# A searched planned order, a root planned step by step, and value projections of 512 columns in a hybrid attention and SSD encoder layer

## The chip, the cores and the metric

The kernel runs on one core of one Trainium2 chip. The core has five instruction queues that run side by side and meet at semaphores: TensorE (PE; its weight loads are shown as PEld), VectorE (DVE), ScalarE (ACT), GpSimd (POOL) and SyncE (SP, which issues the DMAs). The metric is the time of one execution in microseconds (us) on the device. The kernel before takes 1236.46 us, the median of three runs (1235.29 to 1237.94).

## What is computed

One encoder layer on a sequence of 512 tokens with 1024 channels, all in float32:

```
h = layer_norm(x)
proj = h @ w_in                      # q | k | v | z | x_ssd B C | dt | gates
ya = neighbourhood_attention(q, k, v, rpb) @ w_attn_br
xbc = silu(centred_dwconv(x_ssd B C))          # 5 taps, 4096 channels
y = ssd(forward) + ssd(backward) + xs * d_skip  # 8 groups, chunks of 128 tokens
y = y * silu(z);  y = y * rsqrt(mean(y*y over a group's 256) + 1e-5) * ssd_norm_w
ys = y @ w_ssd_br
h = layer_norm(alpha * h + (sigmoid(gate_a) * ya + sigmoid(gate_s) * ys) @ w_o)
h = layer_norm(alpha * h + relu(h @ w_ff1)**2 @ w_ff2)
```

## The kernel before

**Matmuls.** Every large product is done with operands split in two float32r parts, high and low. `mm3` (L305 to L308) issues three matmuls for one tile of 128 contracted channels: high times high (L306), low times high (L307), high times low (L308). Weights come in slabs of 128 x 2048 elements: a DMA into `ws`, a rounded copy into `wh` on ACT and the rest into `wl` on DVE or POOL, with two buffers of each.

**Stages.** First comes the stage that a planner orders: the first norm, the SSD branch over eight groups and the first gates. Then follow the values of the attention (L1053 to L1067), q and k and the attention head by head, the branch projection, the merge, the output projection, and the MLP. The planned stage ends, and the values begin, at 522 us of the profile.

**The planner.** In the planned stage no line issues its instruction at once. `op(engine, us, fn, r, w)` records an operation with its engine, an assumed duration and what it reads and writes. `Plan.order` (L106) then plays these operations as a list schedule: the rank of an operation is the longest assumed path behind it, each engine takes the ready operation of the highest rank, and on PE an operation marked `filler` (the projections) only where no other is ready. A hand-over between engines costs `LAT`, 0.2 us for all engines. An operation marked `lock` on DVE waits for one on POOL to end, and the other way round. `Plan.issue` (L251) plays 100 seeds, each of which multiplies the ranks by a random factor of up to 1.001, keeps the seed whose played end is earliest, and issues the operations in that order. The queues of the engines then run in order: an instruction that waits holds everything behind it on its engine. What is issued after the planned stage is ordered by the compiler's own scheduler.

**A group g of the SSD branch.** Four projections of 128 channels over 512 tokens go to PSUM (`ps_x`, 24 matmuls each, two banks called mm), are convolved (`cv`: ACT one tap, L686; DVE four taps, L694; ACT the silu, L697) and the last two are transposed (`tp_x`, L786). `bc` holds cumulated decays: a DMA from `acs_d` fills it, DVE and POOL subtract (L871), DVE merges the two directions with a predicated copy (L875), ACT takes the exponential (L877), DVE multiplies with `cb` (L879), and PE uses it as weights for `yd` (L885). z is projected with 96 matmuls of 256 columns (`ps_z`), into the same two mm banks. `gated_norm` (L921) multiplies y with z on POOL, squares on ACT, takes the inverse root of four numbers per partition on POOL, scales on ACT, transposes on PE (`tp_y`, L955) and splits into `yTh` (ACT, L958) and `yTl` (DVE, L960). `ssd_branch` multiplies these with `w_ssd_br` (`ps_sbr`) and DVE adds the result into `ysacc` (L981). The transposes `tp_b`, `tp_x` and `tp_y` share two PSUM banks called tr. Names carry the group: `tp_y5_1` is the second transpose of group 5, `cv6_1` the second convolution of group 6.

**The root.** Before, the sixteen instructions of the inverse root are one operation of the plan, with an assumed 3.7 us:

```
op("POOL", 3.7, f_rs, r=[(ssq.name, c) for c in range(NT)], w=[(ssq.name, "r")], lock=True)
```

**The values.** `hBh` and `hBl` are reordered copies of `hTh` and `hTl`, made by 16 DVE copies (L1051). Four slabs of 256 columns are multiplied with them, 4 x 4 x 8 x 3 = 384 matmuls `ps_v`, two blocks of 256 columns to an mm bank; ACT and DVE split each block into `vhl` (L1066, L1067).

Of the kernel before, what the change touches and what calls it, by code (L numbers as in the profile page):

```python
# [19 lines left out]
P = 128  # L20
# [42 lines left out]
SEEDS = 100  # L63
# [7 lines left out]
class Plan:  # L71
# [3 lines left out]
    LAT = 0.2  # L75
# [29 lines left out]
    def order(self, seed=0):  # L105
# [32 lines left out]
        for tag, ts in fixed.items():  # L138
            ts.sort(key=lambda t: first[t])
            for a, b in zip(ts, ts[self.tags[tag]:]):  # L140
                pred[first[b]].update(users[a])
        succ = [[] for _ in ops]
# [14 lines left out]
        for i in reversed(topo):  # L157
            rank[i] = ops[i]["us"] + max((rank[s] + (0 if ops[s]["e"] == ops[i]["e"] else self.LAT)
                                          for s in succ[i]), default=0.0)
# [24 lines left out]
        while done < n:  # L184
            while finish and finish[0][0] <= t:
                _, i = heapq.heappop(finish)
                done += 1
                for s in succ[i]:
                    deg[s] -= 1
                    lat = 0.0 if ops[s]["e"] == ops[i]["e"] else self.LAT  # L190
# [59 lines left out]

    def issue(self):  # L251

        best = None
        for seed in range(SEEDS):
            try:
                o = self.order(seed)
            except AssertionError:
                continue
            if best is None or max(self.end) < best[0]:
                best = max(self.end), o, self.start, self.end  # L260
        self.start, self.end = best[2:]
        for i in best[1]:
            self.ops[i]["fn"]()
# [3 lines left out]
def encoder_layer(ctx, tc, x, w_in, w_attn_br, w_ssd_br, w_o, w_ff1, w_ff2, pcols, rows64,  # L267
# [123 lines left out]
    def by_dir(t, c, g):  # L391
# [7 lines left out]
                 "t1": 2, "ssq": 1, "yTh": 1, "yTl": 1, "gt": 4})  # L399
# [108 lines left out]
    for half in range(2):  # L508
# [9 lines left out]
        for k in range(KD):  # L518
# [8 lines left out]
            if HMB_ENG[half][k] == "ACT":  # L527
                op("ACT", 0.4, lambda k=k, sl=sl, hb_=hb_: a_.activation(
                    hb_()[:, 0], hTh[:, k, sl].bitcast(F32), AF.Identity, bias=nb0[:, k : k + 1]),
                   r=[("hTh", k, half), ("nb0", 0)], w=[(hb_.name, 0)])  # L530
            elif HMB_ENG[half][k] == "DVE":
                op("DVE", 0.28, lambda k=k, sl=sl, bk=bk, hb_=hb_: v_.tensor_scalar(
                    out=hb_()[:, 0], in0=hTh[:, k, sl].bitcast(F32), scalar1=bk, scalar2=None,
                    op0=ALU.subtract), r=[("hTh", k, half)], w=[(hb_.name, 0)], lock=True)
# [4 lines left out]
            op("DVE", 0.43, lambda k=k, tpx=tpx, sl=sl, gk=gk, hb_=hb_: v_.scalar_tensor_tensor(  # L539
# [384 lines left out]
    def gated_norm(g, yz, sz):  # L924
# [12 lines left out]
        box = []  # L937

        def f_rs():
            nc.gpsimd.tensor_scalar(out=ssq(), in0=ssq(), scalar1=1.0 / 256.0, scalar2=None,  # L940
                                    op0=ALU.mult)
            box.append(rsqrt(sbp, ssq(), NT, f"rms{g}", eng=nc.gpsimd))
        op("POOL", 3.7, f_rs, r=[(ssq.name, c) for c in range(NT)], w=[(ssq.name, "r")], lock=True)
        for c in range(NT):
            op("ACT", 0.5, lambda c=c: nc.scalar.activation(yz()[:, c, :], yz()[:, c, :], AF.Copy,
                                                            scale=box[0][:, c : c + 1]),
               r=[(ssq.name, "r"), (yz.name, c)], w=[(yz.name, c)])
# [105 lines left out]
    for s in range(4):  # L1053
        wv = weights([(w_in, 0, OFF_V + s * 256, 256)], KD, 256, f"v{s}")
        for b2 in range(2):
            ps = psx.tile([P, 2, 256], F32, tag="mm", bufs=BANKS["mm"], name=f"ps_v{s}_{b2}")
            for j in range(2):
                bs = slice((2 * b2 + j) * P, (2 * b2 + j + 1) * P)
                for k in range(KD):
                    mm3(ps[:, j, :], hBh[:, k, bs], hBl[:, k, bs],  # L1060
                        wv[0][:, k, :], wv[1][:, k, :], k == 0, k == KD - 1)
            for j in range(2):
                b, prs = 2 * b2 + j, slice(2 * s, 2 * s + 2)
                pv4 = ps[:, j, :].rearrange("p (r h q) -> p r h q", r=2, h=2)
                hi = vhl[:, b, prs, 0:4:3, :]
                nc.scalar.activation(hi, pv4, AF.Copy)  # L1066
                nc.vector.tensor_tensor(out=vhl[:, b, prs, 1:3, :], in0=pv4, in1=hi.bitcast(F32),  # L1067
                                        op=ALU.subtract)
# [422 lines left out]
```

## Time and profile before

| what | value |
|---|---|
| median of three runs | 1236.46 us (1235.29 to 1237.94) |
| the profiled execution | 1234.04 us, of which the span from first to last instruction is 1232.3 us |
| granted TensorE clock, mean | 0.990 |
| PE busy | 1192.6 us, 97% |
| DVE, ACT, POOL busy | 753.9, 557.9, 487.7 us |
| the planned stage | 0 to 522 us |
| the values | 523.2 to 569.5 us |

A matmul of the profile is shown longer than its distance from the next one, since matmuls overlap: 256 columns are shown with 283 ns. The spacing is found by counting matmuls in a stretch in which PE never stops. The granted clock is 1.00 at 2.4 GHz and 0.50 at 1.2 GHz.

### The profile page before, as it was taken

The page shows a single profiled execution, that of the slowest core. Times are in us where ns is not written, and L with a number is a line of the kernel's source. Part 1 is how long each engine was busy: PE and PEld are TensorE (multiplying, and loading weights), DVE is VectorE, ACT ScalarE, POOL GpSimd, SP SyncE. Part 2 cuts the span into 40 slices and gives each one's busy share as a digit, 9 for nine tenths or more (in the row PEclk, how much of TensorE's full clock was granted, in tenths as well). Part 3 has the DMA queues.
Part 4 walks back from the last instruction along what each step waited for, and adds up shares of the span by engine and source line. Part 5 has one row for each costly group of instructions (what it writes and reads, how often), then busy time and mean ns, then how long its engine had stood idle before and what let it go on. Part 6 is the DMA issues. An engine that isn't in the chain of part 4 may idle for free.

```text
span 1232.3 us, 17117 instructions
## 1 busy us (share of the span) xinstructions
PE 1192.6 (97%) x6570; PEld 1029.3 (84%) x6570; DVE 753.9 (61%) x1369; ACT 557.9 (45%) x949; POOL 487.7 (40%) x540
## 2 busy tenths in 40 slices
PE   5999999999999999999999989999999999999997
PEld 5988888988887888799888878889988888888885
DVE  7758586565768486453789975357664343443556
ACT  5557573646545454423667782342232331331510
POOL 1167878686867585403567730015240000000000
PEclk8999999999999999999999999999999999999998
DMA  6153243333333322233333323354213333222401
GB/s 227 52 155 123 89 134 133 108 103 103 103 110 98 124 98 82 88 100 74 93 82 86 83 91 115 103 170 138 69 69 103 103 103 103 90 89 95 151 38 52
DMA packets 126498, 127.22 MB, mean 103 GB/s; under 512 B 22352, under 2 KB 109008, under 8 KB 126416
## 3 DMA queue, kind: packets, MB, share of 16 engines
q1 hardware_dynamic: 126416, 126.13, 32.6%
q8 instruction: 52, 0.85, 0.3%
q14 instruction: 30, 0.25, 0.1%
HBM read 123.88 MB, written 2.23 MB: 102 GB/s over the span
## 4 chain that ended last, share of the span: by engine, by line
PE 79%; DVE 12%; ACT 3%; issue 2%; DMA 2%; POOL 1%; SPq 0%; DVEq 0%; ACTq 0%; POOLq 0%
PE ps_f L308 9%; PE ps_f L307 9%; PE ps_f L306 9%; DVE cv L694 3%; PE ps_x L308 3%; PE ps_x L306 3%; PE ps_x L307 3%; PE yd L885 2%; PE ps_sbr L306 2%; PE ps_z L306 2%; DVE bc L875 2%; PE ps_sbr L308 2%; PE ps_sbr L307 2%; PE ps_z L307 2%; PE ps_z L308 2%
## 5 line engine op out<-in xcount | busy, mean ns | idle before, releaser
L295 ACT ACTIVATE wh_f<-ws_f 128x1024 fp32r<-128x1024 f32 x60 | 60.1, 1052 | 118.6 <-PE ps_f L307 96.4
L694 DVE SCALAR_TENSOR_TENSOR cv<-ps_x,pc,cv 128x510 f32<-128x510 f32 (+1 forms) x128 | 95.5, 748 | 28.0 <-ACT cv L686 24.8
L307 PE MATMUL ps_f<-h1Th,wl_f 128*128 128x512 f32 (+1 forms) x288 | 104.6, 366 | 0.0
L306 PE MATMUL ps_f<-h1Th,wh_f 128*128 128x512 f32 (+1 forms) x288 | 104.4, 366 | 0.0
L308 PE MATMUL ps_f<-h1Tl,wh_f 128*128 128x512 f32 (+1 forms) x288 | 103.1, 367 | 1.0 <-DVE h1Tl L382 1.0
L296 DVE TENSOR_TENSOR wl_f<-ws_f,wh_f 128x1024 fp32r<-128x1024 f32 x60 | 72.8, 1251 | 45.3 <-ACT wh_f L295 45.0
L307 PE MATMUL ps_f<-wh_f,gl 128*128 128x512 f32 x224 | 86.8, 389 | 0.0
L308 PE MATMUL ps_f<-wl_f,gh 128*128 128x512 f32 x224 | 86.5, 389 | 0.0
L306 PE MATMUL ps_f<-wh_f,gh 128*128 128x512 f32 x224 | 86.3, 389 | 0.0
L306 PE MATMUL ps_z<-wh_z,hTh 128*128 128x256 f32 x256 | 75.7, 296 | 2.6 <-DVE cv L694 2.6
L307 PE MATMUL ps_z<-wh_z,hTl 128*128 128x256 f32 x256 | 72.3, 283 | 0.0
L308 PE MATMUL ps_z<-wl_z,hTh 128*128 128x256 f32 x256 | 72.3, 283 | 0.0
L871 DVE TENSOR_TENSOR bc<-bc,amd 128x512 f32<-128x512 f32 x32 | 44.9, 1412 | 37.8 <-DMA bc<-acs_d 30.0
L1364 DVE TENSOR_TENSOR rl<-rl,ps_f 128x512 f32<-128x512 f32 x32 | 21.7, 687 | 69.0 <-ACT rl L1363 68.8
L306 PEld LDWEIGHTS ps_f<-h1Th,wh_f 128*128 128x128 f32 x288 | 54.1, 188 | 8.9
L307 PEld LDWEIGHTS ps_f<-h1Th,wl_f 128*128 128x128 f32 x288 | 54.2, 188 | 8.7
L308 PEld LDWEIGHTS ps_f<-h1Tl,wh_f 128*128 128x128 f32 x288 | 53.3, 188 | 9.8 <-DVE h1Tl L382 1.2
L1363 ACT ACTIVATE rl<-ps_f 128x512 f32<-128x512 f32 x32 | 19.0, 597 | 89.0 <-PE ps_f L308 85.5
L306 PE MATMUL ps_sbr<-yTh,wh_sbr 128*128 128x512 f32 x128 | 56.8, 443 | 1.0 <-DVE ysacc L981 0.9
L306 PE MATMUL ps_x<-hTh,wh_x 128*128 128x512 f32 (+1 forms) x144 | 56.1, 390 | 0.7 <-DVE cv L694 0.7
L306 PE MATMUL ps_x<-hTh,wh_bc 128*128 128x512 f32 (+1 forms) x144 | 56.0, 389 | 0.0
L307 PE MATMUL ps_x<-hTh,wl_bc 128*128 128x512 f32 (+1 forms) x144 | 53.9, 374 | 1.8 <-POOL wl_bc L427 1.8
(300 smaller groups left out, 3723.6 us busy)
## 6 DMA issues: line engine op xcount, KB each, us to landing
ws_f<-in_w_ff SPq DMA_DIRECT2D x32, 1024.0 KB
bc<-acs_d SPq DMA_DIRECT2D x32, 512.0 KB
ws_bc<-in_w_in SPq DMA_DIRECT2D x16, 512.0 KB
ws_x<-in_w_in SPq DMA_DIRECT2D x8, 1024.0 KB
ws_z<-in_w_in SPq DMA_DIRECT2D x8, 1024.0 KB
ws_g<-in_w_in SPq DMA_DIRECT2D x8, 1024.0 KB
ws_sbr<-in_w_ssd_br SPq DMA_DIRECT2D x8, 1024.0 KB
ws_qk<-in_w_in SPq DMA_DIRECT2D x16, 512.0 KB
```

Of the source, the lines that this page charges most:

```text
L295: nc.scalar.activation(hi[:, k], st[:, k], AF.Copy)
L296: (eng[i] if isinstance(eng, tuple) else eng).tensor_tensor(out=lo[:, k], in0=st[:, k], in1=hi[:, k].bitcast(F32), op=ALU.subtract)
L306: nc.tensor.matmul(o, lh, rh, start=start, stop=False)
L307: nc.tensor.matmul(o, ll, rh, start=False, stop=False)
L308: nc.tensor.matmul(o, lh, rl, start=False, stop=stop)
L694: op("DVE", 0.75, lambda j=j, o=o, n=n: nc.vector.scalar_tensor_tensor(out=acc()[:, o], in0=ps()[:, n], scalar=tap(j), in1=acc()[:, o], op ...
L871: op(e, us, lambda d=d, eng=eng, c=c, bc=bc: eng.tensor_tensor(out=bc()[:, d], in0=bc()[:, d], in1=by_dir(amd, c, g)[:, d, :].unsqueeze(2) ...
L875: op("DVE", 0.75, lambda bc=bc: nc.vector.copy_predicated(bc()[:, 0], msk, bc()[:, 1]), r=[(bc.name, 1), ("msk", 0)], w=[(bc.name, 0)], lo ...
L885: nc.tensor.matmul(yd()[:, c % 2, h * HD : (h + 1) * HD], bc()[:, 1, h, :], xtok()[:, c, h * HD : (h + 1) * HD], start=True, stop=True)
L1363: nc.scalar.activation(rl, ps, AF.Relu)
L1364: nc.vector.tensor_tensor(out=rl, in0=rl, in1=ps, op=ALU.mult)
```

## The change

1. `LAT` becomes a table by the engine that hands over: 0.18 us from PE, 0.06 from DVE, ACT and POOL, 0 from SP.
2. The 100 seeds go. `NUDGES` holds ten pairs of a seed and a spread; the ranks are multiplied by the random factors of all ten in turn, and the one order that comes of it is issued. `replay`, a second player that walks a given order in each engine's own sequence with durations lengthened at random, stands in the file and is not called when the kernel is built.
3. Three assumed durations of the first norm become longer (0.4 to 0.51, 0.28 to 0.35, 0.43 to 0.48 us).
4. The root becomes sixteen operations of the plan, 0.29 us each, with one buffer for each of its four tiles where there were two. They are the same sixteen instructions.
5. The values use two slabs of 512 columns, each in two halves of the contraction, in four PSUM banks (so, tr, so, tr): 2 x 2 x 4 x 4 x 3 = 192 matmuls of 512 columns, and 8 blocks of 512 columns to split where there were 16 of 256.

```
-    LAT = 0.2
+    LAT = {"PE": 0.18, "DVE": 0.06, "ACT": 0.06, "POOL": 0.06, "SP": 0.0}
...
-        if seed:
+        for seed, sigma in nudges:
             draw = random.Random(seed)
-            rank = [r * (1 + 0.001 * draw.random()) for r in rank]
+            rank = [r * (1.0 + sigma * draw.random()) for r in rank]
...
-        op("POOL", 3.7, f_rs, r=[(ssq.name, c) for c in range(NT)], w=[(ssq.name, "r")], lock=True)
+        def small(w, f, *r):
+            op("POOL", 0.29, f, r=[(rt[n].name, 0) for n in r], w=[(rt[w].name, 0)], lock=True)
...
-    for s in range(4):
-        wv = weights([(w_in, 0, OFF_V + s * 256, 256)], KD, 256, f"v{s}")
-        for b2 in range(2):
-            ps = psx.tile([P, 2, 256], F32, tag="mm", bufs=BANKS["mm"], name=f"ps_v{s}_{b2}")
...
+    for s in range(2):
+        pss = [psx.tile([P, 512], F32, tag=tag, bufs=BANKS[tag], name=f"ps_v{s}_{b}")
+               for b, tag in enumerate(("so", "tr", "so", "tr"))]
+        for k0 in (0, 4):
+            wv = weights([(w_in, k0 * P, OFF_V + s * 512, 512)], 4, 512, f"v{s}_{k0}")
+            for b in range(4):
+                bs = slice(b * P, (b + 1) * P)
+                for k in range(k0, k0 + 4):
+                    mm3(pss[b], hBh[:, k, bs], hBl[:, k, bs], wv[0][:, k - k0, :], wv[1][:, k - k0, :],
+                        k == 0, k == KD - 1)
```

The added lines move what follows them: in the changed kernel, the lines of the planned stage stand 46 further on (L871 is L917, L875 is L921, L694 is L740), those of the root's end and of `gated_norm` behind it 66 (L955 is L1021, L960 is L1026).

What the new order does on DVE between groups 5 and 6. Before, from the last tap of `cv6_0` on:

```order
L694 SCALAR_TENSOR_TENSOR cv6_0_3561<-ps_x6_0_3512,pc_82,cv6_0_3561 128x510
L694 SCALAR_TENSOR_TENSOR cv6_1_3616<-ps_x6_1_3552,pc_82,cv6_1_3616 128x510
L694 SCALAR_TENSOR_TENSOR cv6_1_3616<-ps_x6_1_3552,pc_82,cv6_1_3616 128x511 x2
L694 SCALAR_TENSOR_TENSOR cv6_1_3616<-ps_x6_1_3552,pc_82,cv6_1_3616 128x510
L875 COPY_PREDICATED bc6_2_3501<-msk_98,bc6_2_3501 128x512
L875 COPY_PREDICATED bc6_3_3509<-msk_98,bc6_3_3509 128x512
L960 SCALAR_TENSOR_TENSOR yTl5_3670<-tp_y5_0_3646,pc_82,yTh5_3660 128x512
L694 SCALAR_TENSOR_TENSOR cv6_2_3668<-ps_x6_2_3608,pc_82,cv6_2_3668 128x510
```

In the changed kernel, the same queue from the late subtractions of `bc6` on:

```order
L917 TENSOR_TENSOR bc6_3_3514<-bc6_3_3514,amd_101 128x512
L917 TENSOR_TENSOR bc6_1_3523<-bc6_1_3523,amd_101 128x512
L740 SCALAR_TENSOR_TENSOR cv6_0_3556<-ps_x6_0_3496,pc_82,cv6_0_3556 128x510
L740 SCALAR_TENSOR_TENSOR cv6_0_3556<-ps_x6_0_3496,pc_82,cv6_0_3556 128x511 x2
L740 SCALAR_TENSOR_TENSOR cv6_0_3556<-ps_x6_0_3496,pc_82,cv6_0_3556 128x510
L921 COPY_PREDICATED bc6_1_3523<-msk_98,bc6_1_3523 128x512
L921 COPY_PREDICATED bc6_3_3514<-msk_98,bc6_3_3514 128x512
L740 SCALAR_TENSOR_TENSOR cv6_1_3597<-ps_x6_1_3552,pc_82,cv6_1_3597 128x510
```

and further down that queue, where group 5 is split:

```order
L849 TENSOR_TENSOR coef6_3722<-dt_100,cbd6_3702 128x16
L851 TENSOR_TENSOR coef6_3722<-coef6_3722,dsk_99 128x16
L740 SCALAR_TENSOR_TENSOR cv6_3_3714<-ps_x6_3_3648,pc_82,cv6_3_3714 128x510
L740 SCALAR_TENSOR_TENSOR cv6_3_3714<-ps_x6_3_3648,pc_82,cv6_3_3714 128x511 x2
L740 SCALAR_TENSOR_TENSOR cv6_3_3714<-ps_x6_3_3648,pc_82,cv6_3_3714 128x510
L1026 SCALAR_TENSOR_TENSOR yTl5_3766<-tp_y5_0_3717,pc_82,yTh5_3756 128x512
L1026 SCALAR_TENSOR_TENSOR yTl5_3766<-tp_y5_1_3727,pc_82,yTh5_3756 128x512
```

The two predicated copies moved from behind `cv6_1` to in front of it, and both splits `yTl5`, which stood on either side of `cv6_2`, moved together behind `cv6_3`.

On PE, where group 5 is transposed. Before, `tp_y5_1` stands within the projection `ps_x6_3`:

```order
L307 MATMUL ps_x6_3_3662<-hTh_69,wl_x6_3531 128x512
L308 MATMUL ps_x6_3_3662<-hTl_70,wh_x6_3521 128x512
L955 MATMUL tp_y5_1_3682<-cst_81,yz5_3473 128x128 x4
L306 MATMUL ps_x6_3_3662<-hTh_69,wh_x6_3521 128x512
L307 MATMUL ps_x6_3_3662<-hTh_69,wl_x6_3531 128x512
L308 MATMUL ps_x6_3_3662<-hTl_70,wh_x6_3521 128x512
L776 MATMUL cb6_3694<-cv6_1_3616,cv6_0_3561 128x128 x4
```

In the changed kernel both transposes stand together within the projection of z:

```order
L352 MATMUL ps_z6_0_3706<-wh_z6_3611,hTh_69 128x256
L353 MATMUL ps_z6_0_3706<-wh_z6_3611,hTl_70 128x256
L354 MATMUL ps_z6_0_3706<-wl_z6_3628,hTh_69 128x256
L1021 MATMUL tp_y5_0_3717<-cst_81,yz5_3484 128x128 x4
L1021 MATMUL tp_y5_1_3727<-cst_81,yz5_3484 128x128 x4
L352 MATMUL ps_z6_0_3706<-wh_z6_3611,hTh_69 128x256
```

Before, `tp_y5_0` and `tp_y5_1` were 15 projection matmuls apart; now they are neighbours, six matmuls of z in.

On PE, the start of the values. Before, two banks side by side:

```order
L306 MATMUL ps_v0_0_4723<-wh_v0_4715,hBh_4697 128x256
L306 MATMUL ps_v0_1_4776<-wh_v0_4715,hBh_4697 128x256
L307 MATMUL ps_v0_0_4723<-wh_v0_4715,hBl_4698 128x256
L308 MATMUL ps_v0_0_4723<-wl_v0_4716,hBh_4697 128x256
L307 MATMUL ps_v0_1_4776<-wh_v0_4715,hBl_4698 128x256
L308 MATMUL ps_v0_1_4776<-wl_v0_4716,hBh_4697 128x256
```

In the changed kernel, four banks side by side:

```order
L352 MATMUL ps_v0_0_4715<-wh_v0_0_4719,hBh_4697 128x512
L352 MATMUL ps_v0_1_4716<-wh_v0_0_4719,hBh_4697 128x512
L352 MATMUL ps_v0_2_4717<-wh_v0_0_4719,hBh_4697 128x512
L352 MATMUL ps_v0_3_4718<-wh_v0_0_4719,hBh_4697 128x512
L353 MATMUL ps_v0_0_4715<-wh_v0_0_4719,hBl_4698 128x512
L354 MATMUL ps_v0_0_4715<-wl_v0_0_4720,hBh_4697 128x512
L353 MATMUL ps_v0_1_4716<-wh_v0_0_4719,hBl_4698 128x512
L354 MATMUL ps_v0_1_4716<-wl_v0_0_4720,hBh_4697 128x512
```

Each stationary tile pair now meets 512 columns of weights at a time, and the first contracted tile serves four blocks of tokens before the second is needed.

## Rows read from the trace of the kernel before

**Rows 1.** The page's first part: busy time, share and instructions of each engine.

```profile
PE 1192.6 (97%) x6570; PEld 1029.3 (84%) x6570; DVE 753.9 (61%) x1369; ACT 557.9 (45%) x949; POOL 487.7 (40%) x540
```

**Rows 2.** Waits of PE: who waited for whom, us in total, times, longest.

```profile
PE tp_h L515 <- DVE xn L486: 10.0, 1, 10.0
PE tp_y L955 <- DVE yTl L960: 2.9, 1, 2.9
PE ps_z L306 <- DVE cv L694: 2.6, 3, 1.5
PE ps_x L307 <- POOL wl_bc L427: 1.8, 1, 1.8
PE tp_x L786 <- DVE yTl L960: 1.8, 1, 1.8
PE ps_v L306 <- ACT wh_v L295: 1.2, 1, 1.2
```

**Rows 3.** PE around 397 us: start, us, instruction, [idle before, releaser].

```profile
396.59 0.39 PE L308 MATMUL ps_x<-hTl,wh_x 128*128 128x512 f32 x1
399.89 1.12 PE L955 MATMUL tp_y<-cst,yz 128*128 128x128 f32 x4 [2.91 <-DVE yTl L960]
```

**Rows 4.** DVE from 379 to 400 us.

```profile
379.58 5.53 DVE L871 TENSOR_TENSOR bc<-bc,amd 128x512 f32<-128x512 f32 x2
...
390.82 3.11 DVE L694 SCALAR_TENSOR_TENSOR cv<-ps_x,pc,cv 128x510 f32<-128x510 f32 x4 [2.70 <-ACT cv L686]
393.85 5.36 DVE L875 COPY_PREDICATED bc<-msk,bc 128x512 f32<-128x512 int32 x2
399.11 0.73 DVE L960 SCALAR_TENSOR_TENSOR yTl<-tp_y,pc,yTh 128x512 fp32r<-128x512 f32 x1
```

**Rows 5.** Stretches: us, busy of each engine (count), granted clock, DMA.

```profile
380.00:400.00 20.00, 17.09 (x79) 13.58 (x78) 17.08 (x14) 12.76 (x23) 15.48 (x22) 0.98 0.22 62
400.00:420.00 20.00, 20.00 (x130) 18.89 (x131) 10.16 (x23) 10.67 (x13) 6.57 (x5) 0.85 0.37 129
```

**Rows 6.** PE around 181 us.

```profile
181.86 1.31 PE L786 MATMUL tp_x<-cst,cv 128*128 128x128 f32 x8 [1.80 <-DVE yTl L960]
```

**Rows 7.** DVE before it.

```profile
177.63 3.54 DVE L875 COPY_PREDICATED bc<-msk,bc 128x512 f32<-128x512 int32 x2
181.07 1.39 DVE L960 SCALAR_TENSOR_TENSOR yTl<-tp_y,pc,yTh 128x512 fp32r<-128x512 f32 x2
```

**Rows 8.** Stretches of 256-column matmuls alone, then of 512-column matmuls alone.

```profile
524.00:564.00 40.00, 40.00 (x336) 40.00 (x334) 18.29 (x33) 10.55 (x20) 0.00 (x0) 1.00 0.30 87
900.00:1000.00 100.00, 100.00 (x443) 82.84 (x442) 46.97 (x54) 32.81 (x45) 6.29 (x3) 1.00 0.30 95
```

**Rows 9.** PE where the planned stage ends and the values begin.

```profile
521.61 0.40 PE L308 MATMUL ps_sbr<-yTl,wh_sbr 128*128 128x512 f32 x1
523.22 0.47 PE L306 MATMUL ps_v<-wh_v,hBh 128*128 128x256 f32 x2 [1.21 <-ACT wh_v L295]
```

**Rows 10.** DVE at the same place.

```profile
522.05 0.69 DVE L981 TENSOR_TENSOR ysacc<-ps_sbr,ysacc 128x512 f32<-128x512 f32 x1 [0.69 <-PE ps_sbr L308]
522.66 0.42 DVE L1051 CAST hBh<-hTh 128x512 fp32r<-128x512 f32 x1
```

**Rows 11.** The splits of the values: durations in ns min/median/max, first and last start.

```profile
L1067 DVE TENSOR_TENSOR vhl<-ps_v,vhl x16: 418/424/427, 532.3 to 573.8; 128x256 fp32r<-128x256 f32 x16
```

**Rows 12.** POOL, the root of the last group, its first and last instruction.

```profile
498.66 0.23 POOL L940 TENSOR_SCALAR ssq<-ssq 128x4 f32<-128x4 f32 x1 [1.03 <-ACT sz L934]
...
503.00 0.20 POOL L329 TENSOR_TENSOR rs_y_rms<-rs_t_rms,rs_y_rms 128x4 f32<-128x4 f32 x1
```

**Rows 13.** Groups by line: count, busy us, mean ns, idle before.

```profile
L875 DVE COPY_PREDICATED bc<-msk,bc 128x512 f32<-128x512 int32 x32 | 48.2, 1536 | 0.2
L871 DVE TENSOR_TENSOR bc<-bc,amd 128x512 f32<-128x512 f32 x32 | 44.9, 1412 | 37.8 <-DMA bc<-acs_d 30.0 <-PE st L849 7.6
...
L877 ACT ACT_TABLE_LOAD x21 | 26.9, 1283 | 1.3 <-DVE bc L875 1.0
```

More of the change, by code (lines that the diff above doesn't have):

```diff
@@ L103, in op, with order @@
                              table=table, filler=filler, at=at))
-    def order(self, seed=0):
+    def order(self, nudges=()):
         ops, n = self.ops, len(self.ops)
@@ L249, in order, with replay @@
         return sorted(range(n), key=lambda i: (start[i], i))
-    def issue(self):
[L253 to L262, printed above, removed]
+    def replay(self, order, seed, spread):
+        ops, n = self.ops, len(self.ops)
+        at = {i: p for p, i in enumerate(order)}
+        pred = [set(p) for p in self.pred]
+        slots = {g: [None] * c for g, c in self.tags.items()}
+        for i in order:
+            for x in ops[i]["tiles"]:
+                u = self.users[x]
+                if i != min(u, key=at.get):
+                    continue
+                s = slots[self.tiles[x].tag]
+                k = min(range(len(s)), key=lambda j: s[j][0] if s[j] else -1.0)
+                if s[k]:
+                    pred[i].update(p for p in s[k][1] if at[p] < at[i])
+                s[k] = (max(self.end[p] for p in u), u)
+        draw = random.Random(seed)
+        queue = {}
+        for i in reversed(order):
+            queue.setdefault(ops[i]["e"], []).append(i)
+        free = dict.fromkeys(queue, 0.0)
+        lock = {"DVE": 0.0, "POOL": 0.0}
+        end, dma, table = [None] * n, 0.0, "sqrt"
+        for _ in range(n):
+            best = None
+            for e, q in queue.items():
+                if not q:
+                    continue
+                i = q[-1]
+                if any(end[p] is None for p in pred[i]):
+                    continue
+                t = max([free[e], ops[i]["at"]] + [
+                    end[p] + (0.0 if ops[p]["e"] == e else self.LAT[ops[p]["e"]]) for p in pred[i]])
+                u = max(t, lock["POOL" if e == "DVE" else "DVE"]) if ops[i]["lock"] else t
+                if best is None or (u, t) < best[:2]:
+                    best = (u, t, e, i)
+            t, _, e, i = best
+            o = ops[i]
+            us = o["us"] * (1.0 + spread * draw.random())
+            if o["table"] and o["table"] != table:
+                us += self.TABLE
+                table = o["table"]
+            if e == "SP":
+                free[e], dma = t + 0.4, max(t, dma) + us
+                end[i] = dma + 2.0
+            else:
+                free[e] = end[i] = t + us
+            if o["lock"]:
+                lock[e] = free[e]
+            queue[e].pop()
+        return max(end)
@@ L263, in issue @@
+    def issue(self):
+        for i in self.order(NUDGES):
             self.ops[i]["fn"]()
@@ L936, in gated_norm @@
                    r=[(yz.name, c)], w=[(sz.name, ("q", c)), (ssq.name, c)])
[L937 to L942, printed above, removed]
-        op("POOL", 3.7, f_rs, r=[(ssq.name, c) for c in range(NT)], w=[(ssq.name, "r")], lock=True)
+        rt = {n: local(f"rs_{n}{g}", f"rs_{n}", [P, NT]) for n in "vnyt"}
@@ new lines, in small @@
+        def small(w, f, *r):
+            op("POOL", 0.29, f, r=[(rt[n].name, 0) for n in r], w=[(rt[w].name, 0)], lock=True)
+        gp_ = nc.gpsimd
+        op("POOL", 0.29, lambda: gp_.tensor_scalar(out=ssq(), in0=ssq(), scalar1=1.0 / 256.0,
+                                                 scalar2=None, op0=ALU.mult),
+           r=[(ssq.name, c) for c in range(NT)], w=[(ssq.name, "m")], lock=True)
+        op("POOL", 0.29, lambda: gp_.tensor_scalar(out=rt["v"](), in0=ssq(), scalar1=EPS, scalar2=None,
+                                                 op0=ALU.add), r=[(ssq.name, "m")],
+           w=[(rt["v"].name, 0)], lock=True)
```

53 lines of the change are left out of this document (32 added, 21 removed).

## The prediction

> **What bounds the kernel now.** I read the busy shares first: PE is busy for 1192.6 of 1232.3 us, and the next engine, DVE, for 61% [rows 1]. The reader is to see that time can leave this kernel in two ways only: less work on PE, or fewer stops of PE. The second view is PE's waits by releaser [rows 2]. Leaving out the 10.0 us of the start, in which the first norm is computed, each wait is small, and nearly all name DVE. The third view is the time around the longest of them. At 396.59 us PE issues its last projection matmul and then stands 2.91 us before `tp_y5_1`, until DVE's `yTl` [rows 3]. DVE's own queue tells why: before that `yTl` come two late subtractions of 5.53 us together and two predicated copies of 5.36 us, with the convolutions between [rows 4]. The split itself takes 0.73 us. The fourth view is the granted clock by stretches: 0.98 in the stretch that holds the stop, 0.85 in the one behind it [rows 5]. Over 20 us each, that is 0.02 x 20 + 0.15 x 20 = 3.4 us of full-speed work lost, which is 6.8 us spent at the lower level of 1.2 GHz. So this one wait costs 2.9 + 3.4 = 6.3 us. The same pattern without a fall of the clock stands at 181 us: PE waits 1.80 us before `tp_x` [rows 6], while DVE finishes two predicated copies of 3.54 us and then the splits [rows 7].
>
> **The values.** The rate of PE is counted in stretches in which it never stops. In 40 us there are 336 matmuls of 256 columns; two of them only reach over the edges, so 40/334 = 119.8 ns each. In 100 us there are 443 of 512 columns, so 100/441 = 226.8 ns each [rows 8]. Before: 384 x 119.8 = 46.0 us. After: 192 x 226.8 = 43.5 us. The change saves 2.5 us, all on PE's path, if nothing else stops PE there. The start does not: PE's first value waits 1.21 us behind the last `ps_sbr` [rows 9]. The releaser is put down to ACT, but DVE adds the last `ps_sbr` from 522.05 and makes the first copy `hBh` from 522.66, ending at 523.08 [rows 10], and that copy is what PE needs. DVE keeps this order, so the 1.2 us stay. Behind it, 16 copies of 0.42 us are due two per contracted tile, 0.84 us; the changed PE order spends 12 x 0.227 = 2.7 us on each of the first two tiles, so the copies stay hidden. The split of a block on DVE took 0.42 us for 256 columns [rows 11] and will take at most twice that (estimate), while a bank is wanted again only after the other three have had their 12 matmuls, 8.2 us. No row shows matmuls that change the bank each time over four banks, so the bounds of this term are no saving at all, if that costs what the wider shape gives, and 2.5 + 1.2 = 3.7 us, if the start closes too. I take 2.5, since before, too, the bank changes within the stretch counted, and PE keeps its rate.
>
> The Trainium skill, TensorE: Matmul & The Clock Gate, section Back-to-back issue gap, gives a spacing of N/2.4 + 2.5 ns for N columns, with hardly any fixed part; by it the two shapes take 109.2 and 215.8 ns, and the values would save 41.9 - 41.4 = 0.5 us. The trace has 11 ns more at both widths, as a part that does not grow with the columns, and I go by the trace.
>
> **The new order, what it removes.** Both transposes of group 5 now stand in the projection of z and both splits behind `cv6_3`, so neither is needed in the middle of a projection while the copies run. I take the 2.9 us and the 3.4 us of clock as gone: 6.3 us; the bounds are 0 (the wait is found again elsewhere) and 6.3. The wait of `tp_x2` goes the same way: before, 18 matmuls of z, 2.2 us, stand between `tp_y1_1` and `tp_x2`, in the change 30, 3.6 us, and on DVE the two copies moved in front of the last convolution. 1.8 us, bounds 0 and 1.8. The three waits of `ps_z` for a convolution, 2.6 us [rows 2], end when DVE has taken the third and fourth convolution out of the mm banks. With the copies earlier and no split between the convolutions these come no later; but what stood in front of them is only shifted. I take half, 1.3 us, bounds 0 and 2.6.
>
> **What it adds.** The two copies that left their place behind `cv6_1` now stand in front of it. `ps_x6_3` needs the bank that `cv6_1` empties, and everything on PE is queued behind it. From the end of `ps_x6_0` PE reaches it after 48 x 0.227 = 10.9 us. In that time DVE has to do `cv6_0` (3.1 us, as `cv6_1` took [rows 4]), the copies (3.5 to 5.4 us [rows 7, 4]) and `cv6_1` (3.1 us): 9.7 to 11.6 us, and more if the late subtractions ahead of `cv6_0` end after `ps_x6_0`. The pattern stands in the steps from group 5 to 6 and from 6 to 7. I take 1.2 us for each, the 0.7 us by which the longer sum fails and 0.5 us for a late subtraction (estimate): +2.4 us; bounds 0, and 6.3 us for each if it grows to what 397 us showed, clock included.
>
> **What it leaves alone.** The root keeps its sixteen instructions: 498.66 to 503.20 us for the last group [rows 12], 4.5 us, where the plan assumed 3.7 and now assumes 4.6. PE projects gates or `ps_sbr` meanwhile; cost 0. If that cover were gone, at most the 0.9 us of the old plan's error would show per group. The new ACT queue has five more table loads in the planned stage, 5 x 1.283 = 6.4 us [rows 13], on an engine that is busy 45% of the time [rows 1]; cost 0, but one of them in front of an exponential that `yd` waits for would cost PE its 1.28 us. The first norm's assumed durations change the order of a few DVE instructions at the start; the waits of 1.8 us and 10.0 us there hang on the load of x and on weights [rows 2]; 0. Behind the values PE, ACT and SP have the same rows.
>
> **The sum.** -2.5 - 6.3 - 1.8 - 1.3 + 2.4 = -9.5 us. The profiled execution took 1234.04 us, so 1224.5 us for one like it; the median of the three runs is 2.4 us above the profiled one, so 1227.0 us.
>
> **The rivals.**
> First, the wait only moves, once: `ps_x6_3` or its like stops for as long as `tp_y5_1` did, and the clock falls again. Then +6.3 stands in place of +2.4, and the time is 1230.9 us. For it: the sum of 9.7 to 11.6 us against 10.9 above. Against it: the splits no longer stand among the convolutions.
> Second, slower: both steps, 5 to 6 and 6 to 7, stop PE for some 2.9 us before the last projection and both let the clock fall, +12.6 us, and the waits of `tp_x` and `ps_z` are only exchanged for others. -2.5 - 6.3 + 12.6 = +3.8 us, 1240.3 us. It decides from the point where copies and late subtractions together take more than some 7 us after `ps_x6_0` has ended (10.9 less 3.1 for `cv6_0`, less 3.1 for `cv6_1`, plus 2.3 us of stop). In the trace they took 5.53 and 5.36 us at their worst [rows 4], so it needs both at their worst twice.
> Third, the order gives nothing: the plan still counts 0.70 us for a subtraction and 0.75 us for a predicated copy, while the trace has means of 1.41 and 1.54 us [rows 13], and random lengthening does not know of that. Then waits are exchanged one for one and the values alone remain: 1234.0 us.
> Fourth, the values save nothing, because a change of bank at each matmul eats what the fewer matmuls give, and the order does as forecast: 1227.0 + 2.5 = 1229.5 us. By the page's formula above the saving would be the 0.5 us, which is nearly this case.
>
> **Chances and range.** Forecast 0.48, with a range of its own from 1219 to 1232 us; first rival 0.20; second 0.13; third 0.12; fourth 0.07. A measurement of this kernel can tell some 0.2%, 2.5 us, from no change: faster means under 1234.0 us, slower over 1238.9. Faster: nearly all of the forecast (0.46), 0.17 of the first, half of the third (0.06), 0.06 of the fourth, 0.75 together. Slower: 0.11 of the second and 0.01 of the third, 0.12. Same: 0.13. The range goes from 1218 us, where waits that I left alone go too, to 1237 us, short of the second rival.
>
> **What would show it.** In the profile of the changed kernel: 192 matmuls `ps_v` within some 43.5 us; no wait of PE for `yTl` over 1 us; a granted clock of 1.00 in every stretch of the planned stage after the first 40 us; PE's waits for `cv` as the longest that are left. Wrong would be a wait of 2 us or more of `ps_x` for `cv` in the last groups with a stretch below 0.95 behind it, or values that still take 46 us.

## The result and the profile after

The changed kernel takes 1220.89 us, the median of 5 runs (1219.99 to 1222.18), against 1236.19 us (1233.52 to 1237.94) for the kernel before, run beside it. The ratio is 0.9886, with a 95% interval from 0.9869 to 0.9904: 12 to 16 us less. The forecast was 1227.0 us, with a range from 1218 to 1237. The direction was right, and the gain is larger than the 9.5 us forecast. The profiled execution took 1219.99 us, with a span of 1217.9 us, 14.4 less than before.

The busy line of the page after, which answers to [rows 1]:

```profile
PE 1185.8 (97%) x6378; PEld 1017.4 (84%) x6378; DVE 725.7 (60%) x1361; ACT 563.2 (46%) x946; POOL 491.6 (40%) x540
```

PE has 192 instructions fewer, as the values should have. DVE has 28 us less to do, though its instructions are nearly the same in number; where that comes from is seen further down.

PE's waits by releaser, which answer to [rows 2] (us in total, times, longest):

```profile
PE tp_h L561 <- DVE xn L532: 9.7, 1, 9.7
PE ps_x L353 <- POOL wl_bc L473: 2.0, 1, 2.0
...
PE ps_x L352 <- ACT wh_bc L470: 1.6, 1, 1.6
...
PE ps_v L352 <- ACT wh_v L341: 1.2, 1, 1.2
...
PE yd L931 <- issue: 0.6, 1, 0.6
...
PE ps_sbr L352 <- DVE ysacc L1047: 0.5, 1, 0.5
...
PE ps_sbr L352 <- ACT yTh L1024: 0.4, 1, 0.4
```

The first three rows are the start. The third is new there; with a wait for `hTl` (0.9 us before, 0.2 now) the start stops PE for 13.5 us in place of 12.7. `ps_v` is the seam, as before. Of the planned stage behind the start only the last three rows are left, 1.5 us. Before, the same list for the stretch from 25 to 520 us came to 10.1 us, with `tp_y`, `ps_z` and `tp_x` at its head. No wait for `yTl` and none for a convolution is left.

The stretches that answer to [rows 5] (us, busy us of PE, PEld, DVE, ACT and POOL with counts, granted clock, DMA share, GB/s):

```profile
380.00:400.00 20.00, 20.00 (x112) 17.33 (x111) 14.09 (x28) 16.81 (x24) 12.34 (x21) 1.00 0.37 119
400.00:420.00 20.00, 20.00 (x133) 17.87 (x133) 11.57 (x18) 8.90 (x13) 17.26 (x16) 1.00 0.31 106
```

The clock is 1.00 where it was 0.98 and 0.85, and PE is busy throughout. DVE in the same step, which answers to [rows 4]:

```profile
382.61 1.35 DVE L921 COPY_PREDICATED bc<-msk,bc 128x512 f32<-128x512 int32 x2
...
400.12 1.40 DVE L1026 SCALAR_TENSOR_TENSOR yTl<-tp_y,pc,yTh 128x512 fp32r<-128x512 f32 x2
```

The pair of copies between these groups took 5.36 us (`bc6_2` and `bc6_3`) and now takes 1.35 (`bc6_1` and `bc6_3`). The reader is to look at POOL for the reason. First POOL of the kernel before, then of the changed one:

```profile
393.42 5.20 POOL L427 TENSOR_TENSOR wl_z<-ws_z,wh_z 128x1024 fp32r<-128x1024 f32 x2 [1.92 <-ACT wh_z L424]
```

```profile
382.59 0.79 POOL L996 TENSOR_SCALAR rs_n<-rs_v 128x4 f32<-128x4 f32 x1
...
386.39 4.77 POOL L473 TENSOR_TENSOR wl_z<-ws_z,wh_z 128x1024 fp32r<-128x1024 f32 x2 [2.10 <-ACT wh_z L470]
```

Before, the copies (393.85 to 399.2) lay beside the split of `wl_z` on POOL (393.42 to 398.6) and ended 0.6 us behind it. In the changed kernel they lie beside the small steps of the root, which stretch a little (0.79 us in place of 0.2), and the split comes later. Over the whole kernel the two groups that answer to [rows 13] became shorter (count, busy us, mean ns, idle before):

```profile
L921 DVE COPY_PREDICATED bc<-msk,bc 128x512 f32<-128x512 int32 x32 | 33.6, 1081 | 0.5 <-POOL bc L917 0.3
L917 DVE TENSOR_TENSOR bc<-bc,amd 128x512 f32<-128x512 f32 x32 | 31.8, 997 | 26.2 <-DMA bc<-acs_d 26.2
```

That is 93.1 us before and 65.4 after, which is the 28 us that DVE lost. The instructions are the same, and nearly all of them lie beside some POOL operation in both kernels. What became fewer are the long ones beside a POOL split of 128 x 1024: of these 64, 17 took over 2 us before, and 2 do now.

The seam on PE, which answers to [rows 9], and a stretch of values alone, to set beside [rows 8]:

```profile
509.66 0.40 PE L354 MATMUL ps_sbr<-yTl,wh_sbr 128*128 128x512 f32 x1
511.27 1.16 PE L352 MATMUL ps_v<-wh_v,hBh 128*128 128x512 f32 x4 [1.21 <-ACT wh_v L341]
```

```profile
512.00:550.00 38.00, 38.00 (x169) 31.44 (x168) 16.78 (x26) 9.42 (x13) 0.00 (x0) 1.00 0.30 89
```

The first value starts at 511.27 us in place of 523.22: the planned stage gave 11.95 us. From the first value to the matmul behind the last it takes 43.62 us in place of 46.18: 2.56 us. These two are the whole difference of the spans but for 0.1 us. The 11.95 us are 10.1 - 1.5 = 8.6 us of waits and 3.4 us of clock, 12.0 together. The 0.8 us by which the waits of the start grew are not in this sum, so it holds to about 1 us.

### The profile page after: what moved, and what is told of

Same layout as the page of the kernel before. It is cut to its first block, busy times and chain, and to the rows that moved or that the text cites. A ratio compares the mean times of both kernels' runs of the same rounds, so it can differ in the third digit from the quotient of the medians.

```text
span 1217.9 us, 16716 instructions
## 1 busy us (share of the span) xinstructions
PE 1185.8 (97%) x6378; PEld 1017.4 (84%) x6378; DVE 725.7 (60%) x1361; ACT 563.2 (46%) x946; POOL 491.6 (40%) x540
## 4 chain that ended last, share of the span: by engine, by line
PE 88%; DVE 5%; ACT 3%; issue 2%; POOL 1%; DMA 1%; SPq 0%; DVEq 0%; POOLq 0%; ACTq 0%
PE ps_f L354 9%; PE ps_f L352 9%; PE ps_f L353 9%; PE ps_x L352 5%; PE ps_x L354 5%; PE ps_x L353 5%; PE ps_z L352 3%; PE ps_z L353 3%; PE ps_z L354 2%; PE yd L931 2%; PE ps_sbr L352 2%; PE ps_sbr L354 2%; PE ps_sbr L353 2%; PE ps_g L352 2%; PE ps_g L353 2%
## 5 line engine op out<-in xcount | busy, mean ns | idle before, releaser
L740 DVE SCALAR_TENSOR_TENSOR cv<-ps_x,pc,cv 128x511 f32<-128x511 f32 (+1 forms) x128 | 95.7, 748 | 25.8 <-ACT cv L732 22.1
L1047 DVE TENSOR_TENSOR ysacc<-ps_sbr,ysacc 128x512 f32<-128x512 f32 x56 | 38.4, 688 | 40.4 <-PE ps_sbr L354 39.9
L1319 POOL TENSOR_TENSOR gt<-gt,ysacc 128x512 f32<-128x512 f32 x8 | 12.8, 1599 | 106.3 <-ACT gt L1059 98.1
```

Of the source, the lines that this page charges most:

```text
L740: op("DVE", 0.75, lambda j=j, o=o, n=n: nc.vector.scalar_tensor_tensor(out=acc()[:, o], in0=ps()[:, n], scalar=tap(j), in1=acc()[:, o], op ...
L1047: op("DVE", 0.69, lambda d=d, ps=ps: nc.vector.tensor_tensor(out=ysacc[:, d, :], in0=ps(), in1=ysacc[:, d, :], op=ALU.add), r=[(ps.name, 0 ...
L1319: nc.gpsimd.tensor_tensor(out=g1, in0=g1, in1=ysacc[:, d, :], op=ALU.mult)
```

## The experiments

The kernels of one group ran on one chip with the kernel before beside them, and each is told by its ratio to that.

**The values alone, and the order alone.** The first is the kernel before with the loops of the values from the changed kernel; the second is the changed kernel with the old loops.

```
-    for s in range(4):  wv = weights(..., KD, 256)      # ps [P, 2, 256], one bank for two blocks
+    for s in range(2):  for k0 in (0, 4): wv = weights(..., 4, 512)   # four banks [P, 512]
```

> The kernel before with the values in 512 columns per matmul and nothing else; its planned order is untouched. My theory: the two parts of the change add up, and this one is worth what the rows of the values gave: 384 matmuls of 256 columns took 46.2 us, 192 of 512 columns take 43.6, so -2.5 us against before (1233.7), with the stop of 2.9 us at tp_y5_1 and the slow stretch behind it unchanged. Rival (the values save nothing alone, because four banks are evicted at a stroke and the next slab waits, and what the changed kernel won here came from the order in front of them): within 1 us of before.

Measured: 1231.91 us, ratio 0.9984 (0.9973 to 0.9996), so -0.5 to -3.3 us. The timed runs alone leave room for the rival's less than 1 us. In the profile the values take 43.64 us, where 46.18 stood before: there the term holds by itself, and the rival falls.

> The changed kernel with the values back at 256 columns per matmul: the order alone. My theory: 2.5 us over the changed kernel (about 1223.4), the planned stage as in the changed kernel: first value matmul near 511 us, no stop at a tp_y or a tp_x. Rival (the two parts help one another, the planned order ends better only with the new values): over the changed kernel by less than 1 or by more than 4 us.

Measured: 1224.63 us, ratio 0.9923 (0.9906 to 0.9941): the order alone is worth 9.5 us, with an interval from 7.3 to 11.6. The values take 46.17 us in it, and the first starts at 511.34, so in the profiles the two parts add up. The timed runs say less: between the ratios 0.9923 and 0.9886 lie 4.6 us, and with both intervals some 1.5 to 7.5 us. That holds the 2.5 us of my theory and also the rival's more than 4.

**The stop at `tp_y5_1` by itself.** In the kernel before, two copies change places with the first `yTl`:

```
  DVE, planned order, step from group 5 to 6:
-   copy bc6_2, copy bc6_3, yTl5_0, ...
+   yTl5_0, copy bc6_2, copy bc6_3, ...      (their exponentials behind them)
```

> The kernel before with one edit in the planned order: the two predicated copies of bc6_2 and bc6_3 stand behind yTl5_0 on DVE and no longer in front of it. My theory: these two copies, 5.4 us beside POOL's wl_z split, are the whole cause of the stop of 2.9 us at tp_y5_1 and of the stretch at 1.2 GHz that follows: both go, -6.3 us; one to two us can come back where ps_z waits for the convolution behind the copies, so -4 to -6.3 us against before. Rival 1 (the stop only moves to the next matmul that waits for DVE, with the slow stretch): within 1 us of before. Rival 2 (the slow stretch has another cause than the stop): -2 to -3 us, and the granted clock stays low near 400 us.

Measured: 1233.59 us, ratio 0.9998 (0.9984 to 1.0012): no gain. My theory fell. As in rival 1 the stop only moved, but the slow stretch did not move with it: the clock from 400 to 420 us is 1.00 here, and 0.91 from 100 to 120 and from 180 to 200 us. PE's waits of this run, then PE where the new one stands:

```profile
PE ps_z L325 <- DVE cv L713: 3.3, 5, 1.5
PE ps_z L325 <- ACT sz L758: 2.4, 1, 2.4
PE tp_x L805 <- DVE yTl L979: 1.9, 1, 1.9
```

```profile
413.50 0.39 PE L325 MATMUL ps_z<-wh_z,hTh 128*128 128x256 f32 x1 [2.40 <-ACT sz L758]
```

The wait for `tp_y` is gone, and 2.4 + 0.7 us stand at `ps_z` in its place. ACT's rows show how it got there:

```profile
405.11 1.28 ACT L716 ACT_TABLE_LOAD   x1 [3.03 <-DVE cv L713]
406.40 0.63 ACT L716 ACTIVATE cv<-cv 128x512 f32<-128x512 f32 x1
407.05 1.28 ACT L896 ACT_TABLE_LOAD   x1
408.34 0.63 ACT L896 ACTIVATE bc<-bc 128x512 f32<-128x512 f32 x1
...
412.85 0.60 ACT L758 ACTIVATE sz<-ps_z 128x512 f32<-128x512 f32 x1
```

The copies still lie beside POOL's split (398.4 to 402.1 us, the split from 396.2 to 401.4) and delay the convolution behind them on DVE. ACT's queue waits for that convolution for 3.03 us, and the `sz` that empties PE's bank stands at the end of ACT's queue. One late pair of copies has several successors, and taking it out of the way of one shows the next.

**The same edit the other way.** In the changed kernel the two copies `bc6_1`, `bc6_3` go directly in front of the first `yTl5`, where POOL splits `wl_sbr`, and their exponentials behind it:

```
-   copy bc6_1, copy bc6_3, cv6_1, cv6_2, ..., cv6_3, yTl5_0
+   cv6_1, cv6_2, ..., cv6_3, copy bc6_1, copy bc6_3, yTl5_0
```

> The changed kernel with one edit in the planned order that goes the other way: the two predicated copies of bc6_1 and bc6_3, which ran at 382.6 us with POOL idle (0.68 us each), stand directly in front of yTl5_0, at 400.1 us, where POOL runs the split of wl_sbr (398.1 to 402.9). My theory: a copy beside a POOL split lasts until the split lets go; the copies take 3 to 5.4 us there, yTl5_0 comes that much later, tp_x6 (403.4 us) and yd6 (405.0 us) wait, and PE stops 1 to 4 us: slower than the changed kernel by 1 to 4 us, and by up to 3.4 us more if the clock falls as it did in before. Rival (the place of the copies does not matter, and the gain came from the order as a whole): within 1 us of the changed kernel, copies 0.7 us each.

Measured: 1229.26 us, ratio 0.9957 (0.9941 to 0.9973). Against the 0.9886 of the changed kernel that is some 9 us more; my range ended at 7.4 us, which the two intervals, some 6 to 11 us, still hold. POOL and DVE, then ACT, then PE:

```profile
399.79 5.24 POOL L492 TENSOR_TENSOR wl_sbr<-ws_sbr,wh_sbr 128x1024 fp32r<-128x1024 f32 x2 [4.48 <-ACT wh_sbr L489]
401.82 3.80 DVE L940 COPY_PREDICATED bc<-msk,bc 128x512 f32<-128x512 int32 x2
405.53 1.39 DVE L1045 SCALAR_TENSOR_TENSOR yTl<-tp_y,pc,yTh 128x512 fp32r<-128x512 f32 x2
```

```profile
405.66 1.15 ACT L942 ACTIVATE bc<-bc 128x512 f32<-128x512 f32 x2 [2.54 <-DVE bc L940]
406.83 1.28 ACT L762 ACT_TABLE_LOAD   x1
408.12 1.15 ACT L762 ACTIVATE cv<-cv 128x512 f32<-128x512 f32 x2
```

```profile
408.80 1.42 PE L851 MATMUL tp_x<-cst,cv 128*128 128x128 f32 x4 [3.51 <-ACT cv L762]
```

```profile
400.00:420.00 20.00, 16.45 (x105) 15.51 (x104) 10.52 (x13) 8.96 (x13) 12.12 (x10) 0.83 0.31 105
```

The copies take 3.80 us beside the split, in place of 1.35 (POOL was not idle at their old place, as I had it, but in the steps of 128x4). The path to PE was again not the one that I had named: ACT waits for the copies, and behind that stands the activation that `tp_x` needs. PE stops 3.51 us and the clock falls to 0.83 of the stretch, which is 3.4 us: 6.9 us together. The first value starts 8.4 us later. Another 1.3 us of that are a wait for `yo` before 363 us, ahead of the edit; a run below, whose planned order is not edited at all, has it too, so it is not the copies' doing. A single pair of copies in a bad place costs this kernel 6.9 us of its profile, most of the 9.5 us that the order gave.

**Is the fall of the clock tied to that one stop?** Run as it was, the kernel before was profiled once more:

> The kernel before once more, unchanged: does the stretch at 1.2 GHz behind the stop at tp_y5_1 (399 us in the first profile) come back? In the profile of the kernel with only the values changed the same stop is there and the clock stays at 2.4 GHz behind it, while the clock falls at 110 us, behind a stop of 1.7 us at ps_z. My theory now: the place wanders from execution to execution among the stops of 1.5 us or more, and the price stays about 3.4 us before the values: the first value matmul starts near 523 us again, wherever the clock falls. Rival (the fall belongs to the stop at tp_y5_1): low at 399 us again, nowhere else between 30 and 520 us.

The stretches and the stop of the kernel with the values alone, and then of this run:

```profile
100.00:120.00 20.00, 18.45 (x100) 16.86 (x100) 16.89 (x29) 14.43 (x23) 12.09 (x16) 0.83 0.40 132
...
400.00:420.00 20.00, 17.57 (x131) 16.71 (x132) 12.63 (x25) 11.68 (x15) 7.67 (x6) 1.00 0.40 128
...
402.30 0.66 PE L955 MATMUL tp_y<-cst,yz 128*128 128x128 f32 x4 [2.89 <-DVE yTl L960]
```

```profile
100.00:120.00 20.00, 18.46 (x100) 16.86 (x100) 16.98 (x30) 14.46 (x23) 12.17 (x16) 0.83 0.42 132
180.00:200.00 20.00, 18.00 (x103) 15.44 (x104) 8.83 (x13) 13.06 (x18) 14.86 (x12) 0.91 0.26 80
...
400.00:420.00 20.00, 17.10 (x99) 15.36 (x98) 15.16 (x26) 13.25 (x16) 8.40 (x4) 0.83 0.25 79
...
404.89 1.12 PE L955 MATMUL tp_y<-cst,yz 128*128 128x128 f32 x4 [2.90 <-DVE yTl L960]
```

This execution took 1240.59 us, with a mean clock of 0.988. Neither theory holds whole. The same stop of 2.9 us at `tp_y5_1` stands in both. In the one the clock stays at 1.00 behind it and falls near 110 us, behind a stop of 1.5 us at `ps_z` (I had written 1.7); in the other it falls at three places. The place wanders, but the price is not fixed either: (0.17 + 0.09 + 0.17) x 20 = 8.6 us here, 3.4 us in the others. The first value starts at 528.19 us, not near 523.

> The changed kernel once more, unchanged, beside the two that follow on the same chip. In three profiles of its planned order the clock never fell between 30 us and the values, in four of the order before it fell there once to three times (3.4 to 8.5 us lost). My theory: no PE stop over 1.5 us stands in this order, so again no fall there, and the first value matmul starts within 0.5 us of 511.3. Rival (the falls are chance and have nothing to do with the order): a stretch at 1.2 GHz between 30 and 511 us, and the first value matmul later by 1.7 us or more.

Measured: 1220.7 us, ratio 0.9883 (0.9860 to 0.9906). The first value starts at 511.43, and in the stretches where the order before lost its clock it is 1.00:

```profile
100.00:120.00 20.00, 19.98 (x127) 17.59 (x126) 17.37 (x35) 12.39 (x21) 17.98 (x20) 1.00 0.42 133
180.00:200.00 20.00, 20.00 (x112) 17.14 (x111) 10.16 (x14) 8.28 (x12) 12.81 (x10) 1.00 0.40 118
...
400.00:420.00 20.00, 20.00 (x134) 17.91 (x133) 11.63 (x18) 8.90 (x13) 17.25 (x16) 1.00 0.33 106
```

So of four profiles with the order of before or nearly that order, all lost clock between 30 us and the values; of six with the changed order none did. The falls go with the order and its stops, but not with one stop, and a stop makes a fall possible, not certain: the order of the old search below, with a stop of 2.5 us at `cb`, lost no clock in its one profile, and the order without nudges lost 1.7 us in its one.

How much of the gain is clock? The mean granted clock of every timed execution beside the experiments is on record. The 41 of the kernel before have 0.9932 (0.989 to 0.996), the 9 of the changed kernel 0.9941 (0.992 to 0.996). Of their spans, 1231.8 and 1218.8 us in the mean, that is 8.4 and 7.2 us lost (in the first two profiles 5.3 and 4.9 us of it lie behind the values). The two are 1.2 us apart, give or take 1.5, and not the 3.4 of the two profiles. The 12 executions of before at 0.996 take 1230.5 us in the mean, the three of the changed kernel at 0.996 take 1218.4. So some 12 us are gained with no difference of the clock, and the execution that the forecast read, at 0.990, is among the quarter of before with the lowest clock.

**The planner without its search, and with the old search.** The changed kernel with an empty list of nudges, and with the best planned end of 100 drawn orders in place of the list:

```
-        for i in self.order(NUDGES):
+        for i in self.order(()):
```

```
+        for seed in range(100):  o = self.order(((seed, 0.001),) if seed else ())
+            if best is None or max(self.end) < best[0]: best = max(self.end), o
```

> The changed kernel with an empty list of nudges: the planner's new costs and lags, no search over orders. My theory: the stops of before came from an order whose costs were too small (0.70 and 0.75 us counted for what takes 1.41 and 1.54); new lags and a root in steps mend a part of it, and the search the rest: between the changed kernel and before with the new values, 1224 to 1230 us, with 3 to 7 us of PE waits in the planned stage. Rival 1 (the costs do it all): within 1.5 us of the changed kernel. Rival 2 (the search does it all): 1231 us or more.

> The changed kernel with the old way to choose among orders: 100 drawn orders, the one whose planned end is earliest, with the new costs and lags. My theory: an early planned end does not keep the stops away, since the plan counts too little for the operations that DVE and POOL do at the same time; it ends like the one order without nudges, 1224 to 1230 us. Rival (any search with the new costs finds an order as good as the changed kernel's): within 1.5 us of the changed kernel.

Measured: 1237.0 us without nudges, ratio 1.0037 (1.0021 to 1.0052), and 1227.22 us with the old search, ratio 0.9950 (0.9935 to 0.9966). Waits of the planned stage without nudges, then with the old search:

```profile
PE yo L944 <- DVE t L956: 5.2, 3, 1.9
PE tp_b L811 <- ACT cv L742: 3.6, 4, 1.0
PE ps_z L351 <- ACT sz L784: 2.4, 1, 2.4
```

```profile
PE tp_b L820 <- ACT cv L751: 2.5, 5, 1.0
PE cb L830 <- DVE bc L933: 2.5, 1, 2.5
```

My theory was wrong on the first: the new costs alone give a worse order than before, even with the 2.5 us of the values in hand, and the time is that of rival 2. On the second it had the time, but not the likeness: the old search with the new costs comes 10 us below the one order, and the listed nudges 6 to 8 us below that. But the search does not do it all. The kernel with the values alone has the same search over the old costs, and its ratio is 0.9984 against 0.9950 here, 4 us. So the costs, the lags and the root in steps, none of which was run by itself, may have a part, or one of the two draws was the luckier; that is not shown. Nor does a run tell what made the listed choice better than the old one, the replay or merely more draws.

What the orders differ in can be told. In the 13 profiles the first value starts between 511.3 and 529.6 us. Take off PE's idle time from 25 us on and the clock lost from 30 us on, and 507.4 to 510.2 us are left in all of them.

**The same edit on w_o.** Since 512 columns paid in the values, the projection w_o was given them too:

```
-        for s in range(4): ... ps_o [P, 256]:  mm3(pss[t], mgh[:, k, ts_], mgl[:, k, ts_], wo[:, k, :])
+        for s in range(2): ... ps_o [P, 512]:  wo = wos[2 * s + k // 4]; mm3(..., wo[:, k % 4, :])
```

> The changed kernel with its edit to the values carried over to w_o: 192 matmuls of 512 columns in two halves of the contraction in place of 384 of 256. My theory: the price of a column falls as it did for the values (119.8 ns for 256 columns, 226.8 ns for 512), so 384 x 0.1198 - 192 x 0.2268 = 2.5 us less than the changed kernel: about 1218.4. Rival (the eviction of 512 columns, 0.7 us in place of 0.4, stands in front of the layer norm of the last two tokens and PE waits for it): within 1 us of the changed kernel.

Measured: 1222.14 us, ratio 0.9908 (0.9894 to 0.9922): no gain over the changed kernel. A stretch of w_o in the changed kernel, then in this one:

```profile
809.00:838.00 29.00, 29.00 (x250) 29.00 (x249) 19.16 (x44) 6.26 (x8) 19.37 (x7) 1.00 0.53 183
```

```profile
809.00:840.00 31.00, 31.00 (x135) 24.91 (x134) 20.19 (x40) 7.13 (x8) 20.86 (x7) 1.00 0.49 173
```

Counted as in [rows 8], 29/248 = 117 ns and 31/133 = 233 ns: the wider matmul costs twice the narrow one, and the two shapes cost the same by the column. From the first matmul of w_o to the end the kernel takes 409.5 us before the edit and 410.5 after. PE has one wait there that the changed kernel has not, for the first layer norm behind w_o:

```profile
PE ps_f L352 <- DVE h1Th L427: 0.9, 1, 0.9
```

That the wider evictions in front of the norm are its cause fits, but was not tested. Two runs asked whether the change of bank is the reason:

> w_o with 512 columns per matmul as in the run before, in another order: twelve matmuls in a row into one bank and then twelve into the other token's, as the values do it, in place of three and three. In the run before a matmul of 512 columns of w_o cost 234 ns, twice the 117 ns of 256 columns, against 227 ns in the values, so it saved nothing. Theory A (the change of bank after three matmuls costs it): 227 ns now, 192 x 0.007 = 1.3 us less than the run before. Theory B (it lies with the operands of w_o or with what else runs there): 234 ns again, no change. In either case within 1.5 us of the changed kernel, since the layer norms behind the wider evictions gave 1.0 us back.

> The changed kernel with the values' loops exchanged: three matmuls into each of the four banks in turn in place of twelve into one. Theory A (the change of bank costs): the median step of a value matmul rises from 227 to 234 ns, 192 x 0.007 = 1.3 us. Theory B (it does not): 227 ns. In both the four banks end together, so that the second half of the values waits for its first eviction, 0.6 to 1.5 us; over the changed kernel by 2 to 3 us under A, by 0.6 to 1.5 under B.

```
-            for k ...: for t in toks: mm3(pss[t], ...)        # w_o: three per bank, then the other
+            for t in toks: for k in range(k0, k0 + 4): mm3(pss[t], ...)     # twelve per bank
-            for b in range(4): for k in range(k0, k0 + 4): mm3(pss[b], ...) # values: twelve
+            for k in range(k0, k0 + 4): for b in range(4): mm3(pss[b], ...) # three
```

Measured: w_o with twelve in a row 1223.9 us, ratio 0.9913 (0.9894 to 0.9932), the values with three in a row 1220.27 us, ratio 0.9888 (0.9864 to 0.9911), beside 0.9883 for the changed kernel on that chip. A stretch of each, w_o and then the values:

```profile
811.00:842.00 31.00, 31.00 (x135) 24.92 (x135) 21.88 (x39) 7.25 (x9) 20.84 (x7) 1.00 0.48 175
```

```profile
515.00:550.00 35.00, 35.00 (x156) 29.01 (x155) 13.32 (x16) 8.20 (x10) 0.00 (x0) 1.00 0.32 93
```

31/133 = 233 ns again, and 35/154 = 227 ns as before the exchange. The change of bank costs nothing, and theory B holds in both. The w_o run stands 3.7 us over the changed kernel, more than expected: by the profile 2.3 of them lie before the values, in a part that the edit does not touch (the first value at 513.75 us, with 1.3 us of waiting for `yo`), and 1.5 behind the start of w_o, 411.0 us from there to the end against 409.5. My 0.6 to 1.5 us for the second half of the values did not come: the last value starts 43.4 us behind the first in either order. Why a column of w_o costs the same at both widths stays open. In its stretch POOL is busy for two thirds of the time and DMA for half, in the values POOL is idle and DMA at 0.3; that is a difference seen, not a cause shown.

No version tried beats the changed kernel by more than its runs scatter.

## Why the prediction came out as it did

**The values.** Forecast -2.5, profile -2.56 us, and by themselves -0.5 to -3.3 us in timed runs. The working from the two rates was right, and so was the step that the seam stays: 1.21 us before and after. The Trainium skill, TensorE: Matmul & The Clock Gate, section Back-to-back issue gap, has a formula, N/2.4 + 2.5 ns, which it gives for an isolated matmul and not for a stream with weight loads; by it, as an estimate, the values would have saved 0.5 us. The trace does not agree: 119.8 and 226.8 ns stand against its 109.2 and 215.8. For w_o, 117 and 233 ns fit its shape, with hardly a fixed part, though not its level.

**The stop and its clock.** Forecast -2.9 and -3.4 us, and both are in the difference of the two profiles. But the reason that I gave, that these 6.3 us hang on that one place, did not hold: taking away that stop alone gave nothing, and the clock falls elsewhere when it does not fall there. What was right is the sum over the order: between the start and the values no stop over 1 us is left, and no clock was lost there in any profile of it. But the 3.4 us are the price of one execution: the profiles of before lost 3.4 us in three cases and 8.5 in one, and over the timed executions the difference of the clock is 1.2 us. That the second profile met the forecast in this term is in part luck.

**`tp_x`.** Forecast -1.8, and the row is gone.

**`ps_z`.** Forecast -1.3, half of 2.6, and all of it is gone. The two waits that I had not listed, `ps_x` for a convolution (0.7) and `yo` (0.6), went as well, 1.3 us more.

**The new waits.** Forecast +2.4 us at `ps_x6_3` and its like, and this is the step that failed. I gave the copies in front of `cv6_1` 3.5 to 5.4 us, the durations of [rows 7, 4]. They take 1.35 us at their new place, with POOL in the small steps of the root, and 1.35 us again in the step from group 6 to 7. The duration was that of a place beside a split on POOL, and I carried it to another place without looking at what POOL does there. DVE and PE of the changed kernel, at `cv6_1` and at the first matmul of `ps_x6_3`:

```profile
385.39 3.10 DVE L740 SCALAR_TENSOR_TENSOR cv<-ps_x,pc,cv 128x510 f32<-128x510 f32 x4 [1.44 <-ACT cv L732]
```

```profile
389.72 0.39 PE L352 MATMUL ps_x<-hTh,wh_x 128*128 128x512 f32 x1
```

`cv6_1` ends at 388.49 us, 1.2 us before PE needs its bank, and no wait came. That is no wide margin. Copies of 5.36 us from 382.61 us, and 3.10 us of `cv6_1` behind them, would have ended at 391.07 us, 1.4 us too late (an estimate from these rows). So the sum of that paragraph was sound, and the duration in it was wrong.

**The sum.** In the profiles -14.4 us against -9.5: 2.6 us more of small waits and 2.4 us that did not come are the 5.0 us between them. The medians differ by 15.3 us, and that is within the interval.

**The rivals.** The first and the second needed the wait at `ps_x6_3`, which is not there. The third, that planned costs too small by half undo the order, is refuted by the order alone, -9.5 us. It was right that the plan's costs alone do not give a good order, as the run without nudges shows. The fourth falls with the values. That the start, the root, the table loads and all behind the values change nothing held, but for 0.8 us more of waits at the start: ACT makes five more loads, no wait of PE names one, and from the matmul behind the last value to the end of the span it is 663 us in both. The sign that waits for `cv` would be the longest left did not come: none is left.

## What to carry to other kernels

Read an operation's duration with the row of the engine that ran beside it, and when it is moved, look up what runs beside the new place before its old duration is carried along. A wait in an order that is full of small waits is not worth its own length: take it away alone and the next in the queue shows, here by way of a third engine; it pays to judge the whole order by the sum of PE's waits. And a price by the column measured in one stage is to be measured again in the stage that it is meant for.

## What was not expected of the hardware

Two predicated copies took 1.35 us beside small POOL operations, and 3.69, 3.80 and 5.36 us beside a POOL split of 128 x 1024, each time ending 0.6 us behind it. Between 30 us and the values the clock fell to 1.2 GHz during stops of PE or up to 2.1 us behind them, stops as short as 1.5 us and twice a few still shorter ones close together. It did so in some executions and not in others, with the same stop. A matmul of 256 columns cost 119.8 ns in the values and z and 117 ns in w_o, one of 512 columns 227 and 233 ns: the one stage pays less for the wide shape, the other pays the same.
